# The gate's column sums as two fp32r products, with their loads moved behind the pieces of w_in

## The chip, the cores and the metric

The kernel runs on one core of a Trainium2 chip. The metric is the device time of one launch in microseconds (us); lower is better. PE is the matrix engine, DVE the vector engine, ACT the scalar engine, SP the queue from which nearly all transfers between memory and the on-chip buffer are issued.

## The reference

One layer of a decoder trunk for 256 positions, D = 2048 and E = 4096, all in fp32:

```python
h = rmsnorm(x, norm_g)
mod = silu(c) @ ada_w + ada_b              # (3 * D): shift, scale, gate
h = h * (1 + scale) + shift
b_gate, c_gate, v, g = split(h @ w_in, 4)  # w_in: (D, 4 * E)
u = causal_depthwise_conv(c_gate * v, conv_w)
y = (b_gate * u * silu(g)) @ w_out         # w_out: (E, D)
return rmsnorm(x + gate * y, final_g)
```

The change concerns `gate`, the last third of `mod`: for each of 2048 columns a sum over the 2048 rows of `ada_w`, weighted with silu(c). It is used only at the end, on the output of w_out.

## The kernel before

**Exact parts.** A large product is done on operands that are split in two. A value is copied to the type fp32r (`hi`, an ACT copy, L314), and what the copy lost is taken by a subtraction on DVE (`lo`, L319). Three products, hi by hi, hi by lo and lo by hi (`product`, L440 to 448), then stand for one. The activations are split likewise (`hT`). An operand of type F32 that is not split is multiplied by PE in full fp32.

**First part of w_in.** Channels 0 to 2047 of each quarter of E are done by `part` (L469): its loads `raw_s` (L487), its products `mm_s`. It runs while the shift and scale columns of ada_w are still being loaded and summed (`ada_piece`, L403; loads `at`, L413; sums on DVE, L427; sums over partitions by transposes `tp_g`, L434). The order of both is written by a planner, `plan`, from costs given by hand.

**Second part of w_in.** Channels 2048 to 4095, in the loop from L573: pairs of channel tiles, four quarters each, and each of these in two pieces of 1 MB. There are 64 pieces. A piece is loaded from SP (`raw`, L579), split on ACT and DVE (L583) and multiplied in 48 products (`mm_b`). Of each of raw, hi and lo there are three buffers, shared with the first part.

**The gate.** 32 steps, (dc, j): four blocks of 512 columns (dc), and in each eight steps of two blocks of 128 rows. `gate_piece` (L546) is called behind every second piece of the second part. It takes one of four `at` buffers, the same that the shift and scale columns use, loads 512 KB into it (`at_g`, L556), and adds the two blocks, weighted, to `gacc` on DVE (L563, L565). Behind the eighth step of a dc, the sum over the 128 partitions is a product with a matrix of ones, and the bias is added:

```python
ps = psum.tile([P, 512], F32, tag="sm", name="ps_gate", bufs=2)
nc.tensor.matmul(ps, ones, ga, start=True, stop=True)
nc.vector.tensor_tensor(out=gate(dc), in0=ps, in1=gate(dc), op=ALU.add)
```

**The output stage.** From L651: four blocks of 512 output columns, for each eight pieces of w_out (`raw_o`, L666) that are split and multiplied (`mm_o`, L629 to 631, 512 columns). In the last block the pieces are first multiplied by the gate (L673); in the others the result is (L692). In front of it SP loads x again and final_g (`big`, L615, L616).

**Order of work.** Outside the start, whose order is pinned, a scheduler orders the instructions of each engine, by a simulated time and by priority. Priority is the place in the program; `with later(GIVE)` puts a block GIVE = 300 instructions further back, which holds for the whole of `gate_sums`, its load too. An instruction of low priority is taken early all the same if its engine has nothing else that is ready; that is how gate loads, which stand in the second part of the program, can be issued during the first. `tc.issue_after(ins)` ties what a block traces on the engine of `ins` behind `ins` in that engine's order, without a semaphore.

Of the kernel before, what the change touches and what calls it, by code (L numbers as in the profile page):

```python
# [8 lines left out]
F32 = mybir.dt.float32  # L9
F32R = mybir.dt.float32r  # L10
AF = mybir.ActivationFunctionType
ALU = mybir.AluOpType

P = 128
# [103 lines left out]
def short_conv_layer(ctx: ExitStack, tc: tile.TileContext, x, c, norm_g, ada_w, ada_b, w_in, conv_w, w_out, final_g, out):  # L118
    nc = tc.nc
# [6 lines left out]
    const = ctx.enter_context(tc.tile_pool(name="const", bufs=1))  # L126
    const.tile([P, 48], F32, tag="line0", name="line0")
    adap = ctx.enter_context(tc.tile_pool(name="adap", bufs=2))
# [10 lines left out]
    def raw_tile(name):  # L139
        return wpool.tile([P, SLOT], F32, tag="raw", name=name, bufs=3)  # L140
# [26 lines left out]
    @contextmanager  # L167
    def later(n):

        now = tc.cur_priority  # L170
        tc.cur_priority = now + n
        yield
        tc.cur_priority = now
# [13 lines left out]
    GIVE = 300  # L187
# [16 lines left out]
    for n, (j, kk) in enumerate(((0, 4), (4, 4), (8, 4), (12, 2), (14, 1), (15, 1))):  # L204
        at = wpool.tile([P, SLOT], F32, tag=("lo", "hi")[n % 2], name="at0", bufs=3)[:, : kk * 2 * NK0 * P]
        at = at.rearrange("p (k s f) -> p k s f", k=kk, s=2)
# [8 lines left out]

    ident = const.tile([P, P], F32, tag="ident", name="ident")
    make_identity(nc, ident)
    ones = const.tile([P, P], F32, tag="ones", name="ones")
    nc.vector.memset(ones, 1.0)
    eps_t = const.tile([P, 1], F32, tag="eps", name="eps_t")  # L220
    nc.vector.memset(eps_t, EPS)

# [11 lines left out]

    def idle(n):
        for _ in range(n):
            nc.tensor.matmul(tp_idle, ident, ones[:, 0:1].to_broadcast([P, 512]), start=True, stop=True)


    warm = const.tile([P, 1], F32, tag="warm", name="warm")  # L240
    tp_idle = psum.tile([P, 512], F32, tag="sm", name="tp_idle", bufs=2)
# [4 lines left out]
    gT = vec[:, 0:KT]  # L246
    bias = vec[:, KT : 3 * KT].rearrange("p (s k) -> p s k", s=2)
    idle(IDLE)


# [3 lines left out]
    for t in range(TT):  # L254
        for dh in range(2):
# [3 lines left out]
            else:  # L259
                nc.vector.scalar_tensor_tensor(  # L260
                    out=junk[:, t], in0=xt[t][dh], scalar=1.0, in1=xt[t][dh], op0=ALU.mult, op1=ALU.mult,
# [72 lines left out]
    def split(raw, n, lo_tag="lo"):  # L334

        return split_lo(raw, n, split_hi(raw, n), lo_tag)
# [4 lines left out]
    gv0 = adap.tile([P, 2, 2 * P], F32, tag="gv", name="gv0")[:, :, 0 : NK0 * P]  # L341
# [6 lines left out]
    def sum0(k, rows, col, halves=(0, 1)):  # L348


        for o in range(2 * NK0):
            if o // NK0 in halves:
                nc.tensor.matmul(
                    sums0[:, o * P : (o + 1) * P], rows[:, o // NK0, (o % NK0) * P : (o % NK0 + 1) * P],
                    col.to_broadcast([P, P]),
                    start=k == ON_PE[0] and o == 0, stop=k is None, skip_group_check=True,
                )

    for k in range(KT):
        c_k = silu_c[:, k : k + 1]  # L360
        at, gv = first_ada[k], gv0
        if k in ON_PE:
# [5 lines left out]
            at, gv = at[:, 1], gv0[:, 1]  # L368
# [2 lines left out]
        else:  # L371
            nc.vector.scalar_tensor_tensor(out=gv, in0=at, scalar=c_k, in1=gv, op0=ALU.mult, op1=ALU.add)
    for half in range(2):
        sum0(None, gv0, ones[:, 0:1], (half,))
    pieces0 = [split(raw0[:, 0 : CT * P], CT * P)]
    hi0 = [split_hi(raw0[:, k * CT * P : (k + 1) * CT * P], CT * P) for k in range(1, NK0)]
    modulate(0, NK0, sums0.rearrange("p (o f) -> p o f", o=2 * NK0)[:, :, 0])
# [7 lines left out]
    def conv(ct, u, cv):  # L385

        nc.scalar.activation(u, cv, AF.Copy, scale=cw[:, 64 + ct : 65 + ct])
        nc.vector.scalar_tensor_tensor(
            out=u[:, 1:T], in0=cv[:, 0 : T - 1], scalar=cw[:, 32 + ct : 33 + ct], in1=u[:, 1:T], op0=ALU.mult, op1=ALU.add
        )  # L390
        nc.vector.scalar_tensor_tensor(
            out=u[:, 2:T], in0=cv[:, 0 : T - 2], scalar=cw[:, ct : ct + 1], in1=u[:, 2:T], op0=ALU.mult, op1=ALU.add
        )

    def split_y(dst, y):
        nc.scalar.copy(dst[:, :, 0, :], y)
        nc.vector.tensor_tensor(out=dst[:, :, 1, :], in0=y, in1=dst[:, :, 0, :].bitcast(F32), op=ALU.subtract)
# [42 lines left out]
    def product(dst, hi, lo, k, i, begins, left, ends):  # L440

        w, h = ((hi, hh_), (hi, hl_), (lo, hh_))[i]

        mm = last_mm[0] = nc.tensor.matmul(dst, w, h[:, k], start=begins and left, stop=ends, skip_group_check=True)  # L444
        if begins and left:
            opener[0] = mm
        elif begins:
            tc.add_manual_dep(mm.ins, opener[0].ins.name, after, reason="the bank's flags are cleared first")
# [91 lines left out]
    def gate(dc):  # L540
        return gates[dc // 2][:, dc % 2, :]
# [1 line left out]
    gate_todo = [(dc, j) for dc in range(4) for j in range(0, KT, 2)]  # L543
    gacc = [None]

    def gate_piece():  # L546
        if not gate_todo:
            return
        dc, j = gate_todo.pop(0)
        at = adap.tile([P, ASLOT], F32, tag="at", name="at_g", bufs=4)  # L550
        at3 = at.rearrange("p (k f) -> p k f", k=2)
        with later(GIVE):
            gate_sums(dc, j, at3)

    def gate_sums(dc, j, at3):
        nc.sync.dma_start(at3, adas[:, j : j + 2, 2, dc * 512 : (dc + 1) * 512])  # L556
        if j == 0:
            gacc[0] = adap.tile([P, 512], F32, tag="gv", name="gacc")
        ga = gacc[0]
        for i in range(2):  # L560
            s = silu_c[:, j + i : j + i + 1]
            if j + i == 0:
                nc.vector.tensor_scalar_mul(ga, at3[:, i, :], s)  # L563
            else:
                nc.vector.scalar_tensor_tensor(out=ga, in0=at3[:, i, :], scalar=s, in1=ga, op0=ALU.mult, op1=ALU.add)  # L565
        if j + 2 == KT:
            ps = psum.tile([P, 512], F32, tag="sm", name="ps_gate", bufs=2)
            nc.tensor.matmul(ps, ones, ga, start=True, stop=True)  # L568
            nc.vector.tensor_tensor(out=gate(dc), in0=ps, in1=gate(dc), op=ALU.add)

    KP = 8
# [1 line left out]
    for ct in range(NS, NCT, 2):  # L573
        for q in QUARTERS:
            bank = psum.tile([P, CT, T], F32, tag="mm", name="mm_b")[:, 0:2]
            col = q * E + ct * P
            for kp in range(0, KT, KP):
                raw = raw_tile("raw")
                nc.sync.dma_start(  # L579
                    raw.rearrange("p (k f) -> p k f", k=KP),  # L580
                    w_in[0, kp * P : (kp + KP) * P, col : col + 2 * P].rearrange("(k p) f -> p k f", p=P),
                )
                hi, lo = split(raw, SLOT)  # L583
                for m in range(2):
                    for i in range(KP):
                        k = kp + i
                        o = slice((i * 2 + m) * P, (i * 2 + m + 1) * P)
                        for j in range(3):
                            product(bank[:, m, :], hi[:, o], lo[:, o], k, j, k == 0 and j == 0, m == 0, k == KT - 1 and j == 2)
                n_piece += 1  # L590
                if n_piece % 2 == 0:
                    gate_piece()
            z = zs[q // 2][:, q % 2]
            if q == 1:
                nc.scalar.copy(z, bank)
                zc = z
            elif q == 2:
                nc.vector.tensor_tensor(out=zc, in0=bank, in1=zc, op=ALU.mult)
                for j in range(2):
                    conv(ct + j, z[:, j, :], zc[:, j, :])  # L600
                u = z
            elif q == 3:
                nc.scalar.activation(z, bank, AF.Silu)
                nc.vector.tensor_tensor(out=u, in0=u, in1=z, op=ALU.mult)
            else:
                nc.vector.tensor_tensor(out=u, in0=bank, in1=u, op=ALU.mult)
                split_y(ys[ct // 2], u)
    while gate_todo:
        gate_piece()


    big = hpool.tile([P, 4, D], F32, tag="big", name="big")
# [38 lines left out]
    for dc in range(4):  # L651
# [10 lines left out]
        for ep in range(n_ep):  # L662
# [7 lines left out]
            if dc == 3:  # L670
# [3 lines left out]
                    out=raw3, in0=raw3, in1=gate(dc).unsqueeze(1).to_broadcast([P, EP, 512]), op=ALU.mult  # L674
# [57 lines left out]
```

## Time and profile before

| | |
|---|---|
| time, median of 3 runs | 913.3 us (912.99 to 914.25) |
| profiled execution: its time, its span | 913.68 us, 911.9 us |
| granted clock of PE, mean | 0.997 |
| moved by DMA | 227.65 MB, mean 250 GB/s |
| gate loads at_g | 32 of 512 KB |
| products ps_gate | 8 records of 128x512, 3.9 us busy |

The span is the time from the first to the last instruction in the trace; the execution's own time has 1.8 us around it. In the profile, Lnnn is a line of the kernel before; "a <- b" in a group names what is written and what is read; "idle before <- releaser" says what ended an engine's idle time. SPq is the queue of SP, PEld the load of weights into PE. A matmul's duration in the records overlaps that of the next one, so what a matmul costs is read from start to start, or from the chain.

### The profile page before, as it was taken

Reading aid. Unit: us, or ns where it says so; the run is one execution under the profiler, and the core shown is the slowest. Engines: PE = TensorE matmul, PEld = TensorE weight load, DVE = VectorE, ACT = ScalarE, POOL = GpSimd, SP = SyncE. Lnnn points to the kernel's source line nnn. Section 1 sums busy time; section 2 is a strip of 40 time slices with the busy share of each in tenths; the row PEclk is TensorE's granted clock in tenths of the full one; section 3 lists DMA queues with packets and bytes.
Section 4 is the critical chain, followed back from the end, with each engine's and each line's share of the span. In section 5 each row is a group of like instructions: output and inputs, shape, how many; then the busy total and the mean of one; then the engine's idle time right before and its main releaser. Section 6 shows DMA issues by size and latency. Waiting matters only on the chain.

```text
span 911.9 us, 16239 instructions
## 1 busy us (share of the span) xinstructions
PE 895.7 (98%) x7047; PEld 858.5 (94%) x7047; DVE 616.2 (68%) x593; ACT 464.6 (51%) x413; POOL 0.7 (0%) x6
## 2 busy tenths in 40 slices
PE   6999999999999999999999999999999999999996
PEld 4999999999999999999999999999999988888885
DVE  4889999989888899765545555545554544555882
ACT  6768856665558756743334433444333333443333
POOL 0000000000000000000000000000000000000000
PEclk9999999999999999999999999999999999999998
DMA  9999999999998698676656665566656486655542
GB/s 309 367 371 353 365 325 351 356 369 352 338 328 275 197 359 301 201 246 197 186 188 197 200 201 186 187 195 200 200 188 188 140 331 231 203 201 186 185 139 92
DMA packets 163752, 227.65 MB, mean 250 GB/s; under 512 B 5680, under 2 KB 104160, under 8 KB 163296
## 3 DMA queue, kind: packets, MB, share of 16 engines
q1 hardware_dynamic: 163552, 226.56, 74.8%
q8 instruction: 55, 0.90, 0.4%
q14 instruction: 17, 0.14, 0.0%
q10 hardware_dynamic: 128, 0.04, 0.0%
HBM read 224.49 MB, written 2.10 MB: 248 GB/s over the span
## 4 chain that ended last, share of the span: by engine, by line
PE 94%; DMA 3%; ACT 1%; SPq 1%; DVE 0%; issue 0%; ACTq 0%
PE mm_b L444 38%; PE mm_s L444 36%; PE mm_o L631 6%; PE mm_o L629 6%; PE mm_o L630 6%; DMA raw_s<-in_sc_w_in_dram 2%; DMA at<-in_ada_w_dram 1%; SPq L210 1%; DMA x<-in_x_dram 1%; ACT hi L314 0%; PE ps_gate L568 0%; PE tp_g L434 0%; ACT acc L465 0%; DVE lo L319 0%; ACT hT L300 0%; SPq L413 0%
## 5 line engine op out<-in xcount | busy, mean ns | idle before, releaser
L444 PE MATMUL mm_s<-hT,hi 128*128 128x256 f32 x2048 | 350.5, 277 | 0.2
L444 PE MATMUL mm_b<-hT,hi 128*128 128x256 f32 x2048 | 348.8, 276 | 0.0
L444 PEld LDWEIGHTS mm_s<-hT,hi 128*128 128x128 f32 x2048 | 308.7, 188 | 1.1 <-ACT hT L300 0.4
L444 PEld LDWEIGHTS mm_b<-hT,hi 128*128 128x128 f32 x2048 | 308.7, 188 | 0.2 <-issue 0.2
L444 PE MATMUL mm_b<-hT,lo 128*128 128x256 f32 x1024 | 282.6, 276 | 0.0
L444 PE MATMUL mm_s<-hT,lo 128*128 128x256 f32 x1024 | 282.2, 277 | 0.2 <-DVE lo L319 0.2
L319 DVE TENSOR_TENSOR lo<-raw,hi 128x2048 fp32r<-128x2048 f32 (+1 forms) x66 | 148.0, 2244 | 136.8 <-ACT hi L314 136.8
L314 ACT CAST hi<-raw 128x2048 fp32r<-128x2048 f32 (+1 forms) x66 | 123.7, 1874 | 200.2 <-PE mm_b L444 156.1
L444 PEld LDWEIGHTS mm_b<-hT,lo 128*128 128x128 f32 x1024 | 192.2, 188 | 0.2 <-issue 0.2
L444 PEld LDWEIGHTS mm_s<-hT,lo 128*128 128x128 f32 x1024 | 191.7, 188 | 0.7 <-DVE lo L319 0.6
L319 DVE TENSOR_TENSOR lo<-raw_s,hi 128x2048 fp32r<-128x2048 f32 (+1 forms) x80 | 147.6, 1850 | 25.6 <-ACT hi L314 24.6
L314 ACT CAST hi<-raw_s 128x2048 fp32r<-128x2048 f32 (+1 forms) x80 | 124.2, 1559 | 72.0 <-PE mm_s L444 59.2
L319 DVE TENSOR_TENSOR lo<-raw_o,hi 128x2048 fp32r<-128x2048 f32 x32 | 73.3, 2292 | 66.3 <-ACT hi L314 66.1
L314 ACT CAST hi<-raw_o 128x2048 fp32r<-128x2048 f32 x32 | 61.0, 1907 | 107.2 <-PE mm_o L631 83.7
L630 PE MATMUL mm_o<-lo,y 128*128 128x512 f32 x256 | 99.7, 391 | 0.0
L629 PE MATMUL mm_o<-hi,y 128*128 128x512 f32 x256 | 99.3, 389 | 0.0
L631 PE MATMUL mm_o<-hi,y 128*128 128x512 f32 x256 | 99.3, 389 | 0.0
L427 DVE SCALAR_TENSOR_TENSOR gv<-at,silu_c,gv 128x512 f32<-128x512 f32 x105 | 78.6, 749 | 2.2 <-DMA at<-in_ada_w_dram 0.3
L465 ACT COPY acc<-mm_s 128x1024 f32<-128x1024 f32 x54 | 54.5, 1012 | 35.9 <-PE mm_s L444 35.9
L630 PEld LDWEIGHTS mm_o<-lo,y 128*128 128x128 f32 x256 | 48.1, 188 | 10.2 <-issue 0.2
L631 PEld LDWEIGHTS mm_o<-hi,y 128*128 128x128 f32 x256 | 48.0, 188 | 10.2 <-issue 0.2
L629 PEld LDWEIGHTS mm_o<-hi,y 128*128 128x128 f32 x256 | 48.1, 188 | 9.9
(89 smaller groups left out, 349.6 us busy)
## 6 DMA issues: line engine op xcount, KB each, us to landing
raw<-in_sc_w_in_dram SPq DMA_DIRECT2D x64, 1024.0 KB, 5.7
raw_s<-in_sc_w_in_dram SPq DMA_DIRECT2D x47, 1024.0 KB, 7.9
raw_o<-in_sc_w_out_dram SPq DMA_DIRECT2D x32, 1024.0 KB, 5.1
at<-in_ada_w_dram SPq DMA_DIRECT2D x114, 256.0 KB, 8.0
raw_s<-in_sc_w_in_dram SPq DMA_DIRECT2D x33, 512.0 KB, 7.1
at_g<-in_ada_w_dram SPq DMA_DIRECT2D x32, 512.0 KB, 7.8
at<-in_ada_w_dram SPq DMA_DIRECT2D x6, 512.0 KB, 9.6
x<-in_x_dram SPq DMA_DIRECT2D x4, 512.0 KB, 6.4
```

The lines of the kernel that those rows point to most:

```text
L210: nc.sync.dma_start(at[:, :, s, :], adas[:, j : j + kk, s, 0 : NK0 * P])
L314: nc.scalar.copy(hi[:, :n], raw[:, :n])
L319: nc.vector.tensor_tensor(out=lo[:, :n], in0=raw[:, :n], in1=hi[:, :n].bitcast(F32), op=ALU.subtract)
L427: nc.vector.scalar_tensor_tensor(out=gv, in0=at4[:, i], scalar=c_k, in1=gv, op0=ALU.mult, op1=ALU.add)
L444: mm = last_mm[0] = nc.tensor.matmul(dst, w, h[:, k], start=begins and left, stop=ends, skip_group_check=True)
L465: nc.scalar.copy(acc[ch, q], bank)
L629: nc.tensor.matmul(po, yh, hi[:, o], start=opens, stop=False, skip_group_check=True)
L630: nc.tensor.matmul(po, yh, lo[:, o], start=False, stop=False, skip_group_check=True)
L631: nc.tensor.matmul(po, yl, hi[:, o], start=False, stop=ct == NCT - 1, skip_group_check=True)
```

## The change

Two things. The sum over partitions is now two fp32r products that accumulate in one bank: `ones` becomes a tile of type fp32r (other uses read it as fp32 by a bitcast), and `gacc` is split in two exact parts in a tile that takes one of the four `at` buffers. And each gate load is tied in SP's order behind the load of the piece of w_in at which `gate_piece` is called, that is, behind every second piece of the second part.

```diff
-    ones = const.tile([P, P], F32, tag="ones", name="ones")
-    nc.vector.memset(ones, 1.0)
+    ones = const.tile([P, P], F32R, tag="ones", name="ones")
+    nc.vector.memset(ones.bitcast(F32), 1.0)
...
-    def gate_piece():
+    def gate_piece(piece):
+
         if not gate_todo:
             return
         dc, j = gate_todo.pop(0)
         at = adap.tile([P, ASLOT], F32, tag="at", name="at_g", bufs=4)
         at3 = at.rearrange("p (k f) -> p k f", k=2)
-        with later(GIVE):
+        with later(GIVE), tc.issue_after(piece.ins):
             gate_sums(dc, j, at3)
...
             ps = psum.tile([P, 512], F32, tag="sm", name="ps_gate", bufs=2)
-            nc.tensor.matmul(ps, ones, ga, start=True, stop=True)
+            parts = adap.tile([P, 2, 512], F32R, tag="at", name="gate_hl", bufs=4)
+            nc.scalar.copy(parts[:, 0], ga)
+            nc.vector.tensor_tensor(out=parts[:, 1], in0=ga, in1=parts[:, 0].bitcast(F32), op=ALU.subtract)
+            for i in range(2):
+                nc.tensor.matmul(ps, ones, parts[:, i], start=i == 0, stop=i == 1)
             nc.vector.tensor_tensor(out=gate(dc), in0=ps, in1=gate(dc), op=ALU.add)
...
-                nc.sync.dma_start(
+                piece = nc.sync.dma_start(
                     raw.rearrange("p (k f) -> p k f", k=KP),
                     w_in[0, kp * P : (kp + KP) * P, col : col + 2 * P].rearrange("(k p) f -> p k f", p=P),
                 )
...
                 if n_piece % 2 == 0:
-                    gate_piece()
+                    gate_piece(piece)
```

More of the change, by code (lines that the diff above doesn't have):

```diff
@@ L236, in idle @@
         for _ in range(n):
-            nc.tensor.matmul(tp_idle, ident, ones[:, 0:1].to_broadcast([P, 512]), start=True, stop=True)
+            nc.tensor.matmul(tp_idle, ident, ones[:, 0:1].bitcast(F32).to_broadcast([P, 512]), start=True, stop=True)
     warm = const.tile([P, 1], F32, tag="warm", name="warm")
@@ L373, in short_conv_layer @@
     for half in range(2):
-        sum0(None, gv0, ones[:, 0:1], (half,))
+        sum0(None, gv0, ones[:, 0:1].bitcast(F32), (half,))
     pieces0 = [split(raw0[:, 0 : CT * P], CT * P)]
@@ L608, in short_conv_layer @@
     while gate_todo:
-        gate_piece()
+        gate_piece(piece)
     big = hpool.tile([P, 4, D], F32, tag="big", name="big")
```

## The prediction, made before the changed kernel was run

> **What bounds the kernel now.** I read the page first (engine shares, chain), then the list of waits of PE, the table by stages, the chain in order of time, and last the views of single lines and tiles. The page and PE's list of waits:
>
> ```profile
> span 911.9 us, 16239 instructions
> PE 895.7 (98%) x7047; PEld 858.5 (94%) x7047; DVE 616.2 (68%) x593; ACT 464.6 (51%) x413; POOL 0.7 (0%) x6
> PE 94%; DMA 3%; ACT 1%; SPq 1%; DVE 0%; issue 0%; ACTq 0%
> ...
> PE tp_v L229 <- DMA rows<-in_ada_b_dram: 4.3, 1, 4.3
> PE tp_v L229 <- DMA rows<-in_c_dram: 4.0, 1, 4.0
> PE mm_s L444 <- DVE lo L319: 0.2, 1, 0.2
> ```
>
> PE is 98% busy and 94% of the chain that ended last is PE. All of its waits but 0.2 us lie in the first microseconds (the transposes tp_v), which the change does not touch. The table by stages says the same of the stretches that the change takes loads from (210 to 353 us) and gives them to (the second part of w_in, 380 to 729 us); its columns are busy time of PE, PEld, DVE, ACT and POOL, then granted clock, DMA share and GB/s:
>
> ```profile
> 20.00:100.00 80.00, 79.56 (x692) 78.63 (x691) 71.73 (x89) 60.84 (x66) 0.00 (x0) 1.00 1.06 365
> 210.00:353.00 143.00, 143.00 (x1252) 142.04 (x1252) 126.75 (x143) 89.42 (x84) 0.00 (x0) 1.00 0.91 309
> 380.00:729.00 349.00, 349.00 (x3076) 348.52 (x3076) 185.15 (x138) 142.21 (x106) 0.00 (x0) 1.00 0.61 194
> 729.00:760.00 31.00, 31.00 (x139) 25.36 (x138) 13.79 (x9) 11.96 (x7) 0.00 (x0) 1.00 0.91 337
> ```
>
> PE is busy for the whole of 210 to 353 us although DVE is at 89% there and the DMA engines at 91%, and for the whole of 380 to 729 us. A busy PE could still be a slow one, so the chain in order of time, whose columns are start, length and piece:
>
> ```profile
> 231.89 70.63 PE mm_s L444 x623
> 302.52 1.72 PE ps_gate L568 x4
> 304.24 76.20 PE mm_s L444 x672
> 380.43 292.17 PE mm_b L444 x2578
> 672.61 0.86 PE ps_gate L568 x2
> ...
> 729.48 0.23 PE mm_o L629
> 729.71 0.23 PE mm_o L630
> 729.94 0.23 PE mm_o L631
> ...
> 751.48 0.86 PE ps_gate L568 x2
> ```
>
> A product of 256 columns takes 70.63/623 = 0.1134 us and 76.20/672 = 0.1134 us while the DMA moves 309 GB/s, and 292.17/2578 = 0.1133 us at 194 GB/s. So neither the heavy loading nor the busy DVE slows PE, and to thin them out between 210 and 353 us is worth nothing. Only work taken off PE, or a new wait of PE, moves the end.
>
> **The change, part by part.**
>
> *The products of the gate's sums.* The rows of L568 in the view by line:
>
> ```profile
> L568 PEld LDWEIGHTS ps_gate<-gacc,ones x8: 187/188/189, 302.2 to 751.3; 128*128 128x128 f32 x8
> L568 PE MATMUL ps_gate<-gacc,ones x8: 590/591/592, 302.4 to 751.7; 128*128 128x512 f32 x8
> ```
>
> There are four such products in the program (one for each 512 columns) and eight records: a full fp32 product goes through PE as two. Its price is what the chain gives, 1.72 + 0.86 + 0.86 = 3.44 us for four, 0.86 us each; the 591 ns of a record overlap the next one. The new form is two fp32r products of 128x512 in place of each. The nearest row is the product of the output stage, fp32r operands of the same shape: starts at 729.48, 729.71, 729.94, 0.23 us each. Two are 0.46 us, so each gate saves 0.40 us and four save **1.6 us**, on the path. Bounds: if the weights of ones are loaded in the open before each (0.188 us by the row above), a pair is 0.84 us and the four save 0.1 us; upward, a pair cannot well be below four products of 256 columns, 4 x 0.1133 = 0.45 us, which gives 1.64 us. I take 1.6, since in the chain of the output stage each 0.23 us product has a weight load of its own that is hidden.
>
> [...]
>
> *The exact parts.* A copy on ACT and a subtraction on DVE for each gate, four of each, priced by the rows of the same shapes and types in the grouped view:
>
> ```profile
> L396 ACT CAST y<-z 128x512 fp32r<-128x512 f32 x8 | 4.9, 614 | 0.0
> L397 DVE TENSOR_TENSOR y<-z,y 128x512 fp32r<-128x512 f32 x8 | 5.5, 685 | 0.0
> ...
> L565 DVE SCALAR_TENSOR_TENSOR gacc<-at_g,silu_c,gacc x60: 739/749/754, 223.3 to 368.2; 128x512 f32<-128x512 f32 x60
> L556 SPq DMA_DIRECT2D at_g<-in_ada_w_dram x32: 367/368/796, 209.9 to 352.6; - x32
> L563 DVE TENSOR_SCALAR gacc<-at_g,silu_c x4: 480/482/485, 222.8 to 332.9; 128x512 f32<-128x512 f32 x4
> ...
> DMA to landing us min/median/max: 3.6/7.8/9.5
> ```
>
> That is 4 x 0.614 = 2.5 us on ACT and 4 x 0.685 = 2.7 us on DVE, both at nothing: from 380 to 729 us ACT is free for 349 - 142 = 207 us and DVE for 349 - 185 = 164 us. Without that cover they would cost 5.2 us.
>
> *The loads and sums that move.* All 32 loads of the gate's columns (512 KB each, 16.8 MB) were issued from 209.9 to 352.6 us, ahead of every w_in load of the second part; now one stands behind every second of the 64 pieces. With them go 60 x 0.749 + 4 x 0.482 = 47 us of DVE. DVE in 380 to 729 us goes from 185 to about 185 + 47 + 3 = 235 of 349 us (67%), less than the 89% at which PE did not wait. The pieces are issued from 357 to 701 us:
>
> ```profile
> L579 SPq DMA_DIRECT2D raw<-in_sc_w_in_dram x64: 367/368/379, 357.4 to 701.1; - x64
> ...
> DMA to landing us min/median/max: 4.3/5.7/9.7
> ...
> SPq L579 <- DVE lo L319: 278.4, 56, 8.7
> SPq L556 <- DVE gacc L565: 16.7, 23, 1.6
> ...
> 543.60 1.91 ACT L314 CAST hi<-raw 128x2048 fp32r<-128x2048 f32 x1 [3.52 <-PE mm_b L444]
> 545.55 2.29 DVE L319 TENSOR_TENSOR lo<-raw,hi 128x2048 fp32r<-128x2048 f32 x1 [3.15 <-ACT hi L314]
> ```
>
> 16.8 MB over 344 us are 49 GB/s more, 194 + 49 = 243 GB/s, where 365 GB/s went through from 20 to 100 us. A gate load waits on SP for one of four at slots, and the next w_in loads are queued behind it; but the SP queue waits for DVE's lo anyway (278 us), and a slot is free 7.8 + 2 x 0.749 = 9.3 us after its load, while the next gate load comes a pair of pieces later, 2 x 48 x 0.1133 = 10.9 us. One slot, at times two, is in use; the new tile of parts, which takes a third until its products have run, leaves one over.
>
> The spare time of a piece follows from the last two rows. The cast waits for PE to free one of three hi buffers, at 543.60; PE comes to the piece so filled two pieces later, at 543.60 + 10.9 = 554.5; its lo ends at 545.55 + 2.29 = 547.8. So 6.6 us of delay on ACT or DVE cost PE nothing. Its load is asked for when a lo frees the slot (547.8), lands 5.7 us later (553.5), and is cast three pieces on, at 543.60 + 16.3 = 559.9: 6.4 us spare; a gate load ahead of it, 0.52 MB at 365 GB/s, takes 1.4 us of these.
>
> *Where the products land in PE's order.* The block is traced with a priority 300 instructions later. For the third gate, traced behind the 48th piece, that is 300/51.5 = 5.8 pieces of 51 instructions and the gate's own: 380.43 + 53.8 x 5.44 = 673 us, and its row stands at 672.61. By the same count the first two, which stood together at 302.52 with their data long there, go to about 500 and 587 us, the third stays near 673 and the fourth near 751. The data of each is complete some 25 to 40 us before that (load issued about three pieces ahead of PE, 9.3 us of landing and sums, 1.3 us of parts), so PE finds the parts ready. The last gate is needed first by the output weights' multiplication:
>
> ```profile
> L673 DVE TENSOR_TENSOR raw_o<-raw_o,gate x8: 2284/2287/2291, 843.4 to 882.2; 128x2048 f32<-128x2048 f32 x8
> ```
>
> Its columns are loaded behind the last piece (701.1), so its sums end near 711 us, 130 us ahead.
>
> *No cost:* the changed type of ones (the idle products and the first sums read the same bytes as fp32).
>
> **Sum.** Profiled execution: 913.68 - 1.6 = 912.1 us, 0.18% less. The profiled execution stands 0.4 us above the median of 913.3 (runs from 912.99 to 914.25); on the median the forecast is **911.7 us**. About 0.2% (1.83 us) is what a measurement of this kernel can tell from no change, so the forecast lies almost on that edge.
>
> **The rivals.**
>
> *A. A queue is held up in the second part (slower).* ACT's copy of a gate's sum stands in ACT's order ahead of a cast, and DVE's sums ahead of a lo. If the scheduler places them as soon as it thinks the load is in, the engine waits for the landing with the split of w_in behind it. From the issue to ready parts there are 7.8 + 1.5 + 0.61 + 0.69 = 10.6 us at the median; over the 6.6 us spare this costs PE 4.0 us for each gate where it happens. With one such wait the kernel is at 911.7 + 4.0 = 915.7, with four at 927.7 us: one decides. [...] Against it: the same sums stood between splits from 222 to 368 us, and neither they nor the casts behind them made PE wait by over 0.2 us. Chance 0.12.
>
> *B. The gain is eaten where the output stage begins (no change).* The thinnest place of the trace is the fifth piece of w_out:
>
> ```profile
> 745.64 1.91 ACT L314 CAST hi<-raw_o 128x2048 fp32r<-128x2048 f32 x1 [8.72 <-DMA raw_o<-in_sc_w_out_dram]
> 747.58 2.29 DVE L319 TENSOR_TENSOR lo<-raw_o,hi 128x2048 fp32r<-128x2048 f32 x1 [8.34 <-ACT hi L314]
> 751.32 1.02 PE L568 MATMUL ps_gate<-gacc,ones 128*128 128x512 f32 x2
> ```
>
> Its lo ends at 749.9, and PE is through with the fourth piece at 751.3: 1.4 us spare. Two gate loads that slip in there (1.05 MB at the 337 GB/s of that stretch, 3.1 us) would cost 3.1 - 1.4 = 1.7 us and leave 913.4 us. Against it: the last gate load is due at 701, 28 us before. Chance 0.07.
>
> *C. The products do not run as fp32r.* Eight full fp32 products would be 8 x 0.86 = 6.9 us, 3.4 us more than now: 916.7 us. Against it: ones and both parts are declared fp32r. Chance 0.02.
>
> **How the numbers follow.** The forecast has 0.79. Around 911.7 its own range is about 0.6 us to each side (the spread of the runs of before), 911.1 to 912.3; the edge of 911.5 lies inside, a little under the middle, and the bounds of the product's price (gain 0.1 to 1.64 us) lean down, the passes up: I give 0.38 to faster and 0.41 to within 0.2%. With B within (0.07), A and C slower (0.14): faster 0.38, same 0.48, slower 0.14. The range for 8 in 10 takes in the forecast with a wider margin below and B: 910.8 to 913.7.
>
> **What would show it.** L568 with eight records at about 0.39 us, in the chain 0.45 us for two; gate loads from about 362 to 701 us; the four pairs near 500, 587, 673 and 751 us; DVE in 380 to 729 us near 235 us; PE full in both stretches, and its list of waits still under 1 us behind the start. The forecast is wrong if PE waits for hi, lo or the parts behind 362 us, if a gap opens near 750 us, or if two records still take 0.86 us.

## The result: 4.6% slower, and the profile after

The changed kernel takes 955.65 us (median of 6 runs, 954.18 to 959.54) against 913.68 us (6 runs, 912.99 to 914.25) of the kernel before: ratio 1.0464, 95% interval [1.0444, 1.0484]. The prediction was 911.7 us in a range of 910.8 to 913.7: it was wrong.

The page of the changed kernel, then PE's list of waits, and last the line of the kernel before that gives its chain by lines:

```profile
span 953.1 us, 16213 instructions
PE 909.4 (95%) x7047; PEld 869.2 (91%) x7047; DVE 614.5 (64%) x597; ACT 465.1 (49%) x417; POOL 0.7 (0%) x6
PE 61%; DMA 24%; DVE 10%; issue 2%; ACT 1%; SPq 1%; ACTq 0%; DVEq 0%
PE mm_s L444 36%; DMA at_g<-in_ada_w_dram 23%; DVE lo L319 7%; PE mm_o L634 6%; PE mm_o L636 6%; PE mm_o L635 6%; PE mm_b L444 5%; DVE gacc L566 3%; PE tp_idle L237 1%; SPq L584 1%; DMA rows<-in_ada_b_dram 1%; PE sum L353 1%; ACT hi L314 0%; PE tp_g L434 0%; PE tp_x L283 0%
...
PE mm_b L444 <- DVE lo L319: 27.7, 22, 2.4
...
PE mm_b L444 38%; PE mm_s L444 36%; PE mm_o L631 6%; PE mm_o L629 6%; PE mm_o L630 6%; DMA raw_s<-in_sc_w_in_dram 2%; DMA at<-in_ada_w_dram 1%; SPq L210 1%; DMA x<-in_x_dram 1%; ACT hi L314 0%; PE ps_gate L568 0%; PE tp_g L434 0%; ACT acc L465 0%; DVE lo L319 0%; ACT hT L300 0%; SPq L413 0%
```

Before, the chain was 94% PE. Now a quarter of it is DMA, nearly all of that the gate loads at_g, and the products mm_b of the second part, which were 38% of the chain, have 5%. PE waits for DVE's lo 22 times, 27.7 us in all. The other part of the loss shows as products that took longer: PE is busy 909.4 us in place of 895.7 with the same 7047 records, and 27.7 + 13.7 = 41.4 us is about the difference of the spans, 41.2. The stages tell where; the columns are those of the table in the prediction:

```profile
210.00:353.00 143.00, 143.00 (x1264) 143.00 (x1263) 89.33 (x87) 90.77 (x85) 0.00 (x0) 1.00 0.65 201
380.00:729.00 349.00, 323.94 (x2743) 319.72 (x2742) 197.91 (x180) 125.86 (x97) 0.00 (x0) 0.98 0.67 214
729.00:760.00 31.00, 28.48 (x235) 28.09 (x233) 17.05 (x14) 11.28 (x10) 0.00 (x0) 0.94 0.63 208
```

From 210 to 353 us everything went as the change says: DVE has 89 us of work in place of 127, the DMA moves 201 GB/s in place of 309, and PE is as full as it was. From 380 to 729 us the trace has 2743 products of PE in place of 3076. Neither DVE (198 of 349 us) nor the DMA (214 GB/s, its engines 67% busy) is full, and yet PE waits: that suggests a loop of waits. The timeline of DVE, and below it that of SP, show one turn of it (start, length, instruction, and in brackets the idle time ahead and what ended it):

```profile
545.03 4.49 DVE L319 TENSOR_TENSOR lo<-raw,hi 128x2048 fp32r<-128x2048 f32 x2
556.15 0.75 DVE L566 SCALAR_TENSOR_TENSOR gacc<-at_g,silu_c,gacc 128x512 f32<-128x512 f32 x1 [6.63 <-DMA at_g<-in_ada_w_dram]
556.81 0.68 DVE L603 TENSOR_TENSOR z<-mm_b,z 128x512 f32<-128x512 f32 x1
557.41 0.74 DVE L566 SCALAR_TENSOR_TENSOR gacc<-at_g,silu_c,gacc 128x512 f32<-128x512 f32 x1
558.07 2.28 DVE L319 TENSOR_TENSOR lo<-raw,hi 128x2048 fp32r<-128x2048 f32 x1
...
547.34 0.37 SPq L584 DMA_DIRECT2D raw<-in_sc_w_in_dram  x1
547.75 0.57 SPq L557 DMA_DIRECT2D at_g<-in_ada_w_dram  x1
...
560.80 0.58 SPq L557 DMA_DIRECT2D at_g<-in_ada_w_dram  x1
```

Count the pieces of w_in from 0, so that gate load k stands behind piece 2k+1. The lo of piece 2k-2 (545.03 to 547.3) frees a raw slot. SP, which waited for that, issues the load of piece 2k+1 at 547.34 and behind it gate load k at 547.75. The load lands 8.3 us later. DVE does the lo of piece 2k-1 and then stands still for 6.63 us, since the scheduler has put the sums of gate load k ahead of the lo of piece 2k. Only when the load has landed and been summed does that lo run, from 558.07 to 560.35, free the next slot, and let SP issue gate load k+1 at 560.80. Every link waits for the one before, and the ring has no slack of its own: its length, not the work of any engine, is the step of two pieces.

```profile
L557 SPq DMA_DIRECT2D at_g<-in_ada_w_dram x32: 567/576/1426, 361.7 to 748.2; - x32
...
  DMA at_g<-in_ada_w_dram: 167.6, 32
...
DMA to landing us min/median/max: 7.0/8.1/9.1
```

In this view of the tile at_g the 32 loads start from 361.7 to 748.2 us: (748.2 - 361.7)/31 = 12.47 us from one to the next, and DVE waited for all 32, 167.6 us in total. PE needs 10.9 us for two pieces (96 products of 0.1133 us in the kernel before). 31 x (12.47 - 10.9) = 49 us, of which the splits' spare takes up the first few; the kernel lost 42. The chain in order of time has the same ring; 27 of the 32 gate loads stand in it, each followed by a lo:

```profile
547.75 8.30 DMA at_g<-in_ada_w_dram
...
558.16 2.20 DVE lo L319
...
560.80 7.54 DMA at_g<-in_ada_w_dram
...
569.56 2.29 DVE lo L319
```

### The profile page after: what moved, and what is told of

It is laid out like the page before. It is cut to its first block, busy times and chain, and to the rows that moved or that the text cites. A ratio compares the mean times of both kernels' runs of the same rounds, so it can differ in the third digit from the quotient of the medians.

```text
span 953.1 us, 16213 instructions
## 1 busy us (share of the span) xinstructions
PE 909.4 (95%) x7047; PEld 869.2 (91%) x7047; DVE 614.5 (64%) x597; ACT 465.1 (49%) x417; POOL 0.7 (0%) x6
## 4 chain that ended last, share of the span: by engine, by line
PE 61%; DMA 24%; DVE 10%; issue 2%; ACT 1%; SPq 1%; ACTq 0%; DVEq 0%
PE mm_s L444 36%; DMA at_g<-in_ada_w_dram 23%; DVE lo L319 7%; PE mm_o L634 6%; PE mm_o L636 6%; PE mm_o L635 6%; PE mm_b L444 5%; DVE gacc L566 3%; PE tp_idle L237 1%; SPq L584 1%; DMA rows<-in_ada_b_dram 1%; PE sum L353 1%; ACT hi L314 0%; PE tp_g L434 0%; PE tp_x L283 0%
## 5 line engine op out<-in xcount | busy, mean ns | idle before, releaser
L444 PE MATMUL mm_b<-hT,hi 128*128 128x256 f32 x2048 | 358.4, 280 | 0.0
L444 PE MATMUL mm_b<-hT,lo 128*128 128x256 f32 x1024 | 289.2, 282 | 27.7 <-DVE lo L319 27.7
L444 PEld LDWEIGHTS mm_b<-hT,hi 128*128 128x128 f32 x2048 | 315.4, 191 | 0.0
L444 PEld LDWEIGHTS mm_b<-hT,lo 128*128 128x128 f32 x1024 | 196.1, 191 | 32.2 <-DVE lo L319 32.0
L566 DVE SCALAR_TENSOR_TENSOR gacc<-at_g,silu_c,gacc 128x512 f32<-128x512 f32 x60 | 45.0, 749 | 155.5 <-DMA at_g<-in_ada_w_dram 154.9
L636 PEld LDWEIGHTS mm_o<-hi,y 128*128 128x128 f32 x256 | 48.1, 188 | 10.1
```

Of the source, the lines that this page charges most:

```text
L636: nc.tensor.matmul(po, yl, hi[:, o], start=False, stop=ct == NCT - 1, skip_group_check=True)
```

## The experiments

Theory L is this ring. Against it stood D (16.8 MB more in the second part, so that w_in itself comes late), S (the split of the sum: ACT's copy, DVE's subtraction, the third `at` slot) and the plain view that 47 us of added DVE work are too much there.

**One half of the change at a time.** Only the fp32r products:

```diff
-        with later(GIVE), tc.issue_after(piece.ins):
+        with later(GIVE):
```

> The changed kernel with its two fp32r products, but the gate loads not tied to the pieces of w_in. Theory L (a closed loop: DVE takes the gate's sums k ahead of the split lo of piece 2k, the load k is issued only when lo of piece 2k-2 has freed a raw slot, and 0.4 us of issue + 8.4 landing + 1.7 sums + 2.2 lo = 12.7 us for each pair of pieces is longer than PE's 10.9): no loop here, so 913.7 - 1.6 = 912.1 us, ratio 0.998, and two records of the product 0.45 us in the chain. Rival D (16.8 MB more in the second part make the loads of w_in late): the same 912.1, since the loads are back in the first part. Rival S (the split's ACT copy, DVE subtraction and third at slot hold up the queues): near 955 us.

Measured: 912.43 us, ratio 0.9989, 95% interval [0.9980, 0.9998]. The chain in order of time, the pieces of the four products:

```profile
302.37 0.93 PE ps_gate L573 x4
...
671.86 0.24 PE ps_gate L573
...
672.22 0.23 PE ps_gate L573
...
750.11 0.46 PE ps_gate L573 x2
```

0.93 + 0.47 + 0.46 = 1.86 us in place of 3.44: 1.58 us saved. S, which expected near 955 us, falls. The other half alone, the tie with the full fp32 products:

```diff
-        with later(GIVE):
+        with later(GIVE), tc.issue_after(piece.ins):
             gate_sums(dc, j, at3)
...
-            gate_piece()
+            gate_piece(piece)
```

> The kernel before with its full fp32 products, and the gate loads tied behind every second piece of w_in. L: the loop alone, 955.7 + 1.6 = about 957 us, DVE waiting for at_g about 32 times, 5 us each. D: the same, about 957. S: near 914 us.

Measured: 955.09 us, ratio 1.0458 [1.0444, 1.0473]. DVE's waits:

```profile
DVE gacc L565 <- DMA at_g<-in_ada_w_dram: 153.7, 28, 7.5
DVE gacc L563 <- DMA at_g<-in_ada_w_dram: 14.6, 4, 4.4
```

The whole loss is the tie's. The 1.6 us of the products do not show between this kernel and the changed one (955.09 and 955.65 us): with the ring in front, PE is not what is waited for.

**The same loads, the sums further back.** This tells L from D, for the bytes and the ties of the loads stay as they are, and the sums alone are tied further back in DVE's order:

```diff
-        nc.vector.tensor_tensor(out=lo[:, :n], ...)
+        last_lo[0] = nc.vector.tensor_tensor(out=lo[:, :n], ...)
...
-        with later(GIVE), tc.issue_after(piece.ins):
+        with later(GIVE), tc.issue_after(piece.ins), tc.issue_after(last_lo[0].ins):
```

> The changed kernel, loads tied as in it, but the sums of each gate load placed in DVE's order behind the split lo of the piece that the load stands behind, that is two lo further back. L: the load then has two more lo's time before DVE asks for it, the loop is open, 912 us, DVE waits for at_g under 5 us in all. D: the same bytes at the same places, so about 955 us, with ACT waiting for raw. A third view, that 47 us more of DVE work are too much for the second part: also about 955 us.

Measured: 912.58 us, ratio 0.9988 [0.9979, 0.9997]. The loads, their landing, and the stage:

```profile
L558 SPq DMA_DIRECT2D at_g<-in_ada_w_dram x32: 567/576/1516, 361.6 to 700.3; - x32
...
DMA to landing us min/median/max: 6.6/7.4/8.9
...
380.00:729.00 349.00, 349.00 (x3071) 348.58 (x3070) 229.14 (x203) 143.82 (x111) 0.00 (x0) 1.00 0.75 238
```

All 16.8 MB and all the sums are in the second part, the DMA moves 238 GB/s and DVE works 229 us, more than the 198 us of the changed kernel, and PE is busy for 349.00 of 349.00 us. D falls, and so does the view that DVE has too much to do. D's own sign, ACT waiting for raw, is there in the changed kernel:

```profile
ACT hi L314 <- DMA raw<-in_sc_w_in_dram: 50.1, 14, 5.2
```

In e3 this wait is not in the list: the loads of w_in came late because the lo ahead of them did, not because of the bytes. A load still takes 7.4 us; nobody asks for it before. Three of the 32 gate loads also came one piece later in SP's order than in the changed kernel; in the next run SP's order of these loads is the same as there.

How far back is needed? One lo, by L, since then the lo that frees the slot for load k+1 no longer waits for load k:

```diff
-        last_lo[0] = nc.vector.tensor_tensor(out=lo[:, :n], ...)
+        last_lo[:] = last_lo[1:] + [nc.vector.tensor_tensor(out=lo[:, :n], ...)]
...
-    last_lo = [None]
+    last_lo = [None, None]
```

(against e3: the list holds the last two lo, and the sums go behind the older one).

> The changed kernel with the sums of each gate load one lo further back in DVE's order: ahead of the lo of its own piece, behind that of the piece before. L: lo of piece 2k no longer waits for load k, so the loop closes over two pairs instead of one, about 0.4 + 8.4 + 1.5 + 2 x 2.3 = 15 us against 21.8: open, 912.5 us; DVE still waits for at_g now and then, PE does not. If only the full two lo's of e3_sums_behind_lo were enough: between 912.5 and 955 us.

Measured: 912.25 us, ratio 0.9984 [0.9975, 0.9993].

```profile
L558 SPq DMA_DIRECT2D at_g<-in_ada_w_dram x32: 570/576/1309, 361.7 to 700.5; - x32
...
DMA to landing us min/median/max: 6.7/7.4/9.1
...
380.00:729.00 349.00, 349.00 (x3071) 348.60 (x3071) 229.00 (x204) 143.90 (x111) 0.00 (x0) 1.00 0.76 238
```

DVE has no wait for at_g left in its list, which is better than the "now and then" expected. One place in DVE's order is worth 43 us.

**Is it the ring, or each wait by itself?** The sums of every second load were put behind the lo as in e3, the others left where the changed kernel has them (against e3):

```diff
-        with ..., tc.issue_after(last_lo[0].ins):
+        with ..., tc.issue_after(last_lo[0].ins if j % 4 else piece.ins):
```

> The changed kernel, where the sums of every second gate load are put behind the lo of their own piece (as in e3_sums_behind_lo) and the others stay where the changed kernel has them. L: sixteen waits of DVE for at_g remain, each 1.7 us longer than PE's pace allows, but the chain from one to the next is broken, a pair without it catches up, and 6.6 us of spare take up 1.7: 912.5 us, PE with no wait. If each wait costs by itself (43 us / 32): 16 x 1.3 = 21 us, 934 us.

Measured: 912.24 us, ratio 0.9984 [0.9974, 0.9993]. DVE's waits:

```profile
DVE gacc L567 <- DMA at_g<-in_ada_w_dram: 17.5, 11, 2.4
DVE gacc L565 <- DMA at_g<-in_ada_w_dram: 4.6, 4, 2.3
```

DVE still waits 15 times, 1.5 us each, with a lo behind it, and PE never waits for that. The waits are also shorter than the 5.2 us each (167.6/32) of the changed kernel. A wait in the wrong place costs nothing while the spare is renewed in between; thirty-two that each start the next cost 43 us.

**An earlier load does not help when the sums move along.** The load one piece earlier:

```diff
-                if n_piece % 2 == 0:
+                if n_piece % 2 == 1:
```

> The changed kernel with each gate load one piece earlier: behind the first piece of a pair in place of the second. In DVE's order the scheduler has moved the sums up by one lo as well (the sums of a load behind piece n stand ahead of lo of piece n-1, as in the changed kernel). L: the load is issued when lo of piece n-3 is done, the next but one lo waits for it, the loop is the same 12.5 us for a pair: 955 us. If what counts were how early the load stands in SP's queue: 5.4 us less wait for each, 912.5 us.

Measured: 955.99 us, ratio 1.0463 [1.0447, 1.0478].

```profile
L557 SPq DMA_DIRECT2D at_g<-in_ada_w_dram x32: 367/576/585, 356.8 to 741.6; - x32
...
380.00:729.00 349.00, 318.12 (x2738) 312.92 (x2736) 200.38 (x184) 127.43 (x97) 0.00 (x0) 1.00 0.67 214
```

The load starts 5 us earlier (356.8 for 361.7) and the step is (741.6 - 356.8)/31 = 12.41 us. The stage also settles a side question: in the changed kernel the granted clock fell to 0.98 from 380 to 729 us, but this kernel is as slow at a clock of 1.00 there, so the clock is not what cost the time. PE is busy 904.7 us here and waits 33.9 us for lo, against 909.4 and 27.7 us in the changed kernel: the sum is nearly the same.

**Shorter links.** Half of each load, and then half of the sums; both kernels leave out half of the gate's rows and serve for the time alone. If the ring is the bound, the time follows its length:

```diff
-        nc.sync.dma_start(at3, adas[:, j : j + 2, 2, ...])
+        nc.sync.dma_start(at3[:, 0:1], adas[:, j : j + 1, 2, ...])   # the sums add at3[:, 0] twice
```

> The changed kernel with only the first of the two blocks of 128 rows in each gate load (256 KB in place of 512 KB), added twice, so that DVE's work and the order are the same; half of the gate's rows are left out. L: the landing is shorter by 0.26 MB at 350 GB/s = 0.75 us, the loop 11.9 us instead of 12.6, the loss 31 x 1.0 us less 6.6 us of spare = 24 us: about 935 us. D: half of the bytes, half of the loss, about 933 us (not told apart from L by this run alone; by the waits it is: L has DVE waiting for at_g, D has ACT waiting for raw). If the landing does not get shorter, L gives 955 us.

Measured: 918.75 us, ratio 1.0062 [1.0039, 1.0084].

```profile
L557 SPq DMA_DIRECT2D at_g<-in_ada_w_dram x32: 565/573/812, 361.4 to 709.9; - x32
...
DMA to landing us min/median/max: 6.1/6.6/8.6
```

The expected 935 us was a miss in one number: the landing became shorter by 8.1 - 6.6 = 1.5 us, not by 0.75. With 1.5 the ring is 12.5 - 1.5 = 11.0 us, hardly longer than PE's pace; measured (709.9 - 361.4)/31 = 11.24. Half of the bytes gave back 37 of 43 us, which D's half of the loss does not fit. DVE waits for at_g 126.7 us, and ACT for raw 29.6 us, in place of 50.1.

```diff
-        for i in range(2):
+        for i in range(1):     # of the sums of a gate load
```

> The changed kernel with only the first of the two additions for each gate load (the load is whole; half of the gate's rows are left out of the sum). L: a link of the loop is shorter by 0.75 us, 12.53 - 0.75 = 11.8 us for a pair against PE's 10.9, 31 x 0.9 - 6.6 us of spare = 21 us: 933 us, and the step between gate loads on SP 11.8 us. D (the bytes): 955 us, all bytes are still moved.

Measured: 932.11 us, ratio 1.0206 [1.0178, 1.0235].

```profile
L557 SPq DMA_DIRECT2D at_g<-in_ada_w_dram x32: 567/576/1426, 361.9 to 722.3; - x32
...
DMA to landing us min/median/max: 6.6/7.9/9.0
```

Expected 933, with a step of 11.8 us; the step is (722.3 - 361.9)/31 = 11.63. One DVE instruction of 0.75 us less in each turn, with the same bytes, and 23.5 us of the loss are gone: 31 x 0.75 = 23.3. The four runs lie between 929.55 and 935.88 us, so that the two agree to a few tenths is luck. Together, with the step taken from the first and last start of the loads:

| kernel | step of the gate loads, us | 31 x (step - 10.93), us | time, us | above 912.3 |
|---|---|---|---|---|
| e3, sums behind lo | 10.93 | 0 | 912.58 | 0.3 |
| e8, one lo | 10.93 | 0 | 912.25 | 0 |
| e4, half load | 11.24 | 9.6 | 918.75 | 6.4 |
| e7, one sum | 11.63 | 21.7 | 932.11 | 19.8 |
| e5, first of pair | 12.41 | 45.9 | 955.99 | 43.7 |
| changed kernel | 12.47 | 47.7 | 955.65 | 43.3 |

The last column follows the third, less 2 to 4 us that the spare of the splits could take up (less than the 6.6 us of the prediction; why was not tried). The step is that of the profiled execution and the time the median of all runs; with the profiled executions' own times (917.01, 929.55, 956.17 and 954.91 us) it is 2 to 5 us. That a slower stage has a longer step would hold for any cause; that the ring sets the step is shown by e4 and e7, where one link was made shorter, and by e3 and e8, where it was opened.

The kernels with products of fp32r and no ring (e1, e3, e6, e8; 912.2 to 912.6 us) beat the kernel before by 0.1 to 0.2% and the changed one by 4.5%. The best of them do not differ by more than their intervals.

## Why the prediction was wrong

**What held.** PE bounds the kernel (94% of the chain before), and to relieve 210 to 353 us gains nothing: PE is busy for 143.00 of 143.00 us there in both kernels. The products save 1.58 us by the chain (1.6 predicted), and the forecast ratio of 0.998 lies in the intervals of e1, e3, e6 and e8 (e1 at 0.9989 [0.9980, 0.9998]). With the sums one or two lo further back the rest came out too: DVE 229 us (235 predicted), 238 GB/s (243), and in e3 the pairs of products at 497, 585, 672 and 750 us (500, 587, 673, 751):

```profile
497.01 0.23 PE ps_gate L574
...
584.54 0.23 PE ps_gate L574
...
672.07 0.23 PE ps_gate L574
...
750.32 0.46 PE ps_gate L574 x2
```

The forecast sets "the passes" against the bounds that lean down. No run shows such a term; the chains show 0.86 us for a full fp32 product, which has two records, and in e1 0.46 to 0.47 us for the pair of fp32r products in its place.

**The step that failed** is the cover of the moved loads: "6.6 us of delay on ACT or DVE cost PE nothing", and in rival A "the same sums stood between splits from 222 to 368 us, and neither they nor the casts behind them made PE wait by over 0.2 us". Two things were missed.

First, the prediction wrote down both halves of the ring and did not join them. It said that SP waits for DVE's lo anyway (278 us), that the gate load stands behind that wait, that it lands 7.8 us later, and that DVE may take the sums ahead of a lo. That is a circle: 0.4 + 8.3 + 1.5 + 2.3 = 12.5 us against 10.9, with the landing of the turn shown above (by the median of 8.1 it is 12.3, and single DVE instructions of other work stand in between). All of these terms stood in the prediction, with 7.8 us for the landing and without the 0.4 of an issue: 11.6 us, already more than the pace. A spare of 6.6 us covers a delay that comes once, or that the pace gives back; it does not cover 1.6 us that come again in every turn.

Second, the evidence from before did not carry over. There the gate loads ran ahead of the sums by free `at` slots (the first was issued at 209.9 us, its sum began at 222.8) and were tied to no lo, so an early place of the sums in DVE's order did no harm; e1, without the tie, has five waits of DVE for at_g, 7.8 us in all, and PE has none for lo. With the tie an early place closed the ring. That it would put the sums so early was not checked against anything; I took "lower priority" for "later".

**Rival A** named the right wait, DVE's sums ahead of a lo while their load has not landed, but not the ring: it priced 4.0 us for each of four products, at a chance of 0.12. The loss is 1.3 us net for each of 32 loads. "One decides" does not hold for every such wait either: e6 has fifteen, of 1.5 us each, and loses nothing (912.24 us). Rivals B and C did not come up: no stretch near 750 us holds PE up in e3, where PE's list of waits has only the two of the start, 4.3 and 4.0 us; and two of the new products take 0.46 us in its chain, where two in full fp32 would be 1.72 us.

Why the scheduler puts the sums ahead of a lo for which their load has not yet landed was not tried. A landing that its simulated time takes to be shorter than 8 us would do it, but no run here shows that.

## What to carry to other kernels

When a change ties a load behind another one, follow the tie round: what does that other load wait for, and does the user of the new load stand ahead of it in an engine's order, as the sums did here in DVE's, which stood still for 6.63 us with the next lo behind them? If the walk comes back to its start, add up the links and compare with the pace of the bounding engine for the same work, here 12.5 us against 10.9; the spare counted once here, the excess in every turn. The cure was cheap: one place further back in the user's order opened the ring (912.25 us), while an earlier load, with its user moved along, did not (955.99 us).

## What the runs showed of the hardware

A gate load that is shorter by 0.26 MB lands 1.5 us sooner (medians 8.1 and 6.6 us, changed kernel against e4). If the bytes alone did that, it is an estimated 175 GB/s, half of the 350 GB/s that the estimate of 0.75 us went by and that the DMA moved from 100 to 210 us in the changed kernel. In both kernels a load of 1 MB is issued 0.4 us ahead of the gate load (547.34 and 547.75 us in the changed kernel) and the next one mostly 2 to 4 us behind it (549.54; 554.82 behind 552.43 in e4). In e3 that next one comes some 5 us behind (552.06 behind 547.03), and the whole 512 KB land in 7.4 us. So the bytes alone do not set the landing; how much is due to them and how much to the loads around was not separated.
